# A decoder layer in three-product fp32: one set of PSUM pools to the end, output tiles paired q with 4 + q, second norm two products later, operands ahead of weight parts, three parts ahead

## The chip, the cores and the metric

The kernel runs on one core of a Trainium2 chip. The metric is the device time of one launch in microseconds (us), the median over several runs. Engines are called as the profile calls them: PE is TensorE (matmuls), PEld its weight loads, DVE is VectorE, ACT is ScalarE, POOL is GpSimd, SP the engine that issues the DMAs. SBUF is the on-chip memory; PSUM holds eight banks of 128 x 512 fp32 into which PE writes its sums.

## The reference

One hybrid decoder layer on x of 1024 positions by 1024 channels, everything in fp32:

```python
def layer(x, ...):
    h = x + hybrid_mixer(rms_norm(x, norm1_g), w_in, conv_w, conv_norm_g, ret_norm_g, w_out)
    h = h + sq_relu_mlp(rms_norm(h, norm2_g), w_up, w_down)
    return rms_norm(h, final_norm_g)

def hybrid_mixer(u, w_in, conv_w, conv_norm_g, ret_norm_g, w_out):
    z = u @ w_in                                  # 1024 x 3584
    # 512 columns: short causal convolution, gated, group norm
    # 4 heads of 128: rotary, chunkwise retention, norm, swish gate
    return concat([y_conv, y_ret], -1) @ w_out    # 1024 x 1024

def sq_relu_mlp(u, w_up, w_down):                 # 1024 -> 4096 -> 1024
    hdn = relu(u @ w_up)
    return (hdn * hdn) @ w_down
```

## The kernel before

**Precision.** Every large matmul runs on operands that are split in two: hi is the value rounded to the matmul's fp32r type, lo is the rest. A product is hi x hi + hi x lo + lo x hi, so three matmuls (128 x 128 times 128 x 512) where one would do. On top of that the large products are done by Strassen's scheme in Winograd's form: seven products of half the size in place of eight, at the price of additions before (on operands) and after (on results).

**Weights.** A weight piece `r` (128 x 4 x 128) comes by DMA from SP's queue. `split_piece` (line 168) makes two tiles of it: `wh`, a cast on ACT, and `wl`, the difference `r - wh`, on DVE (on POOL in part of the first stage). Both come from a pool `wp` of four buffers each. `prepare()` (line 180) takes the next entry of a list and appends the finished piece to `parts`; each product pops one. How many pieces are split ahead of the product that uses them is set by the early calls `prepare(2)` (lines 297 and 381): four ahead, which is as many as there are buffers. One product of 12 matmuls uses one piece.

**Order.** Each engine executes its own list in the order in which the program emits it; the order is written out by hand through a planner that estimates each engine's clock (`Engine`, `slot`, `tick`), and after a product's matmuls the program emits what the other engines do with it.

**Output projection (`group(j)`, line 1060).** Four groups j, each with output tiles j and 4 + j, eight steps. A step has 12 matmuls into one bank from `pm` or `pr`, four banks each. `out_evac` adds the finished bank into `x2[i]` (DVE, `x <- x,b`), squares it into the sums of the second norm, and begins the normalised operand `un[i]`. `group_todo` lists what else is emitted: the operands `U` of the up-projection and Strassen's sums on them. `prepare` stands at steps 4 to 7, ahead of `out_evac`.

**Change of pools.** After the fourth group the pools `pm` and `pr` are closed and three others take the eight banks: `pu` (two, up products), `pd` (four, down products), `pn` (two: the rows `r_half` of the second norm, kept through the MLP).

**MLP.** 64 up-projection row tiles are made in pairs of products. 14 early products (line 1251, `at` = 0 to 13) come first, two pairs interleaved; beside them the list `rest` emits what is left of the operands. `token_roots`, `rnorms` and `spread` turn the sums of squares into `r_half`; until then finished results wait. Then come the cycles of `jobs` (line 1301): up products (line 403, `b <- U,wh`) alternate with down products (line 1277, `b <- V,wh`), 12 matmuls each. An up result goes through relu, square and the norm factor (tiles `t`, on DVE, ACT and POOL) and becomes the operand `V` of a down product. `down_take` adds a finished down bank into quarters of `x2`.

**Pairs of output tiles.** Strassen's scheme for the down-projection is kept in a basis in which two output tiles form a 2 x 2 block: `x2[2q]` and `x2[2q+1]`. `new_basis(i)` (line 1004) changes the residual into that basis with two subtractions on POOL. Since SBUF is full, finished tiles are written out to DRAM (`put_aside`) and read again (`fetch_back`). `new_basis(1)` runs among the output groups, `new_basis(7)`, `(5)` and `(3)` at early products 7, 8 and 9, on tiles read back.

**End.** After the last cycle the basis is changed back and the last piece of the down-projection is done without Strassen (`last_mm`, line 1382), into four banks `zs` from `pn`, `pr` and `pm`; then the final norm.

Of the kernel before, what the change touches and what calls it, by code (L numbers as in the profile page):

```python
# [40 lines left out]
IN_END = [22, 23]  # L41
# [38 lines left out]
def hybrid_layer(  # L80
# [29 lines left out]
    banks_ = ctx.enter_context(ExitStack())  # L110
    pm = banks_.enter_context(tc.tile_pool(name="pm", bufs=4, space=PSUM))
    pr = banks_.enter_context(tc.tile_pool(name="pr", bufs=4, space=PSUM))
# [268 lines left out]
    prepare(2)  # L381
# [529 lines left out]
    for half in range(2):  # L911
        for f, (z, banks, pieces) in ends.items():
            for c in range(2):
# [8 lines left out]
                if half:  # L922
                    prepare()
# [80 lines left out]
    def new_basis(i):  # L1004


        for f, part in ((i - 1, hs[1]), (i, hs[0])):
            pool.tensor_sub(x2[f][:, part], x2[f][:, part], x2[i][:, hs[1]])
# [29 lines left out]
    def group_todo(j):  # L1038
# [12 lines left out]
        if j < 3:  # L1051
# [5 lines left out]
            todo[15] = [lambda: put_aside(4 + j)]  # L1057
        return todo

    def group(j):  # L1060
# [3 lines left out]
        for s, (i, c, half) in enumerate(steps):  # L1064
# [13 lines left out]
            if half:  # L1078
                prepare()
            if c:  # L1080
                out_evac(i, half, banks[i, half])
            for t in todo.get(8 * j + s, []):
                t()
            if s == 2 and j in (1, 2):
                down.fetch(4)
# [6 lines left out]
    todo[16] += [lambda: new_basis(1)]  # L1092
    todo[17] += [lambda: put_aside(0), lambda: put_aside(1)]
    todo[24] += [lambda: put_aside(2)]
    for j in range(4):
        group(j)
    banks_.close()
    pm = ctx.enter_context(tc.tile_pool(name="pu", bufs=2, space=PSUM))
    pr = ctx.enter_context(tc.tile_pool(name="pd", bufs=4, space=PSUM))
    pn = ctx.enter_context(tc.tile_pool(name="pn", bufs=2, space=PSUM))  # L1100
# [131 lines left out]
    def lo22(j):  # L1232
# [3 lines left out]
        todo[32] + call(hi22, 3),  # L1236
        todo[33] + todo[34] + hi("t2", 3),
        lo("t2", dve, 3) + hi("t3", 3) + call(lo22, 3),
# [4 lines left out]
        call(new_basis, 7),  # L1243
        call(new_basis, 5),
        call(new_basis, 3),
        [lambda: v_split(early, 1, 0)],
        [lambda: v_split(early, 1, 1)],
        [],
        [],
    ]  # L1250
    for at, (n, p) in enumerate((n, p) for n in MLP_ORDER for p in range(EARLY)):
# [3 lines left out]
        prepare()  # L1255
        for f in rest[at]:
            f()
        put_now()
        early[p].take(n, b)
        if at == 3:  # L1260
            roots = [token_roots([sums_[h]], rtok[:, 4 * h : 4 * h + 4]) for h in range(2)]
        if at == 5:
            wides = [rnorms(r) for r in roots]
        if at == 8:
            r_half[:] = [spread(w, pn) for w in wides]
# [14 lines left out]
    def down_take(n, h, bs):  # L1280
        for i, b in enumerate(bs):
            q = 2 * h + i
            quads = [x2[2 * q + f][:, sl] for f in range(2) for sl in hs]
# [17 lines left out]
    def jobs(b, old, new):  # L1301

        todo = []
        for k, n in enumerate(DOWN_ORDER):
# [8 lines left out]
            if b == NBLK - 2:  # L1313
# [3 lines left out]
                if k == 6:  # L1317
                    for q in range(4):
                        x = x2[2 * q + 1]
# [28 lines left out]
    for q in range(4):  # L1348
        pool.tensor_add(x2[2 * q][:, hs[1]], x2[2 * q][:, hs[1]], x2[2 * q + 1][:, hs[1]])
# [3 lines left out]
    TE = T - P  # L1353
# [210 lines left out]
```

## Time and profile before

| | |
|---|---|
| median of 3 runs | 1070.92 us (1070.82 to 1071.99) |
| profiled execution | 1070.03 us |
| its span | 1068.1 us |
| PE busy | 1054.8 us, 99% of the span, 4860 matmuls |
| DVE busy | 870.8 us, 82% |
| POOL busy | 561.6 us, 53% |
| ACT busy | 463.6 us, 43% |
| granted clock of PE | 9 tenths or more in each of 40 slices |

The span is one profiled execution from its first to its last instruction; the two microseconds beside it are in no row. PE is busy in 99% of the span, and its matmuls are pipelined: one starts about 0.23 us after the one ahead of it, although each lasts 0.39 us. So a delay is read from the distance of starts: two successive rows of one matmul each that start more than 0.23 us apart have a gap between them. A row with x2 or x3 merges successive matmuls.

The stages on the time axis: input projection, convolution and retention up to about 330 us, output projection 330 to 432, early MLP products 432 to 470, cycles of up and down products 470 to 1011, last down piece and final norm to 1068.

### The profile page before, as it was taken

Reading aid. Unit: us, or ns where it says so; the run is one execution under the profiler, and the core shown is the slowest. Engines: PE = TensorE matmul, PEld = TensorE weight load, DVE = VectorE, ACT = ScalarE, POOL = GpSimd, SP = SyncE. Lnnn points to the kernel's source line nnn. Section 1 sums busy time; section 2 is a strip of 40 time slices with the busy share of each in tenths; the row PEclk is TensorE's granted clock in tenths of the full one; section 3 lists DMA queues with packets and bytes.
Section 4 is the critical chain, followed back from the end, with each engine's and each line's share of the span. In section 5 each row is a group of like instructions: output and inputs, shape, how many; then the busy total and the mean of one; then the engine's idle time right before and its main releaser. Section 6 shows DMA issues by size and latency. Waiting matters only on the chain.

```text
span 1068.1 us, 13853 instructions
## 1 busy us (share of the span) xinstructions
PE 1054.8 (99%) x4860; PEld 879.2 (82%) x4860; DVE 870.8 (82%) x1231; ACT 463.6 (43%) x906; POOL 561.6 (53%) x381
## 2 busy tenths in 40 slices
PE   9999999999999999999999999999999999999997
PEld 8888888788888888788788888888888888888886
DVE  7446546799998665799999989999899899899955
ACT  8211445673437444443343433343443434334453
POOL 6334324367854233559458267277186295384552
PEclk9999999999999999999999999999999999999999
DMA  7121122122223733051221211211301201200204
GB/s 276 65 58 42 38 80 70 63 95 80 69 69 129 256 115 123 11 187 39 61 59 49 79 31 50 90 30 50 99 21 50 89 21 49 90 21 19 69 30 158
DMA packets 39685, 82.25 MB, mean 77 GB/s; under 512 B 4544, under 2 KB 5696, under 8 KB 39616
## 3 DMA queue, kind: packets, MB, share of 16 engines
q1 hardware_dynamic: 39328, 80.85, 23.5%
q8 instruction: 38, 0.62, 0.2%
q10 hardware_dynamic: 288, 0.52, 0.1%
q14 instruction: 31, 0.25, 0.1%
HBM read 71.92 MB, written 9.44 MB: 76 GB/s over the span
## 4 chain that ended last, share of the span: by engine, by line
PE 90%; DVE 6%; ACT 2%; issue 1%; POOL 1%; DVEq 0%; ACTq 0%; POOLq 0%
PE b L403 55%; PE b L1277 23%; PE b L357 4%; PE b L1386 4%; DVE t L74 1%; DVE wl L74 1%; DVE x L74 1%; DVE m L74 1%; ACT h L74 1%; DVE q L74 1%; DVE V L74 1%; PE b L339 0%; PE b L595 0%; PE b L1436 0%; PE b L246 0%
## 5 line engine op out<-in xcount | busy, mean ns | idle before, releaser
L74 ACT CAST wh<-r 128x512 fp32r<-128x512 f32 x286 | 176.6, 620 | 326.4 <-PE b L403 134.4
L403 PE MATMUL b<-U,wh 128*128 128x512 f32 x1024 | 315.8, 390 | 2.0 <-DVE x L74 1.2
L74 DVE TENSOR_TENSOR wl<-r,wh 128x512 fp32r<-128x512 f32 x250 | 232.8, 933 | 89.0 <-ACT wh L74 87.8
L74 POOL TENSOR_TENSOR r<-r,r 128x512 f32<-128x512 f32 x136 | 210.2, 1548 | 114.1 <-DVE wl L74 66.1
L1277 PE MATMUL b<-V,wh 128*128 128x512 f32 x784 | 242.0, 389 | 0.7 <-POOL V L74 0.4
L403 PEld LDWEIGHTS b<-U,wh 128*128 128x128 f32 x1024 | 191.7, 188 | 43.2 <-issue 2.4
L74 DVE TENSOR_TENSOR x<-x,b 128x512 f32<-128x512 f32 (+1 forms) x312 | 195.5, 673 | 28.8 <-PE b L1386 14.3
L403 PE MATMUL b<-U,wl 128*128 128x512 f32 x512 | 199.2, 389 | 0.0
L1277 PEld LDWEIGHTS b<-V,wh 128*128 128x128 f32 x784 | 147.1, 188 | 32.4 <-POOL V L74 0.9
L74 POOL TENSOR_TENSOR t<-t,t 128x512 f32<-128x512 f32 x70 | 106.3, 1523 | 96.4 <-ACT t L74 50.4
L1277 PE MATMUL b<-V,wl 128*128 128x512 f32 x392 | 152.5, 389 | 0.0
L74 POOL TENSOR_TENSOR wl<-r,wh 128x512 fp32r<-128x512 f32 x36 | 51.4, 1432 | 119.3 <-ACT wh L74 116.5
L403 PEld LDWEIGHTS b<-U,wl 128*128 128x128 f32 x512 | 96.1, 188 | 19.9
L403 PE MATMUL b<-uh,wh 128*128 128x512 f32 x304 | 102.3, 396 | 0.0
L403 PE MATMUL b<-ul,wh 128*128 128x512 f32 x304 | 100.5, 390 | 0.0
L403 PE MATMUL b<-uh,wl 128*128 128x512 f32 x304 | 100.2, 389 | 0.0
L1277 PEld LDWEIGHTS b<-V,wl 128*128 128x128 f32 x392 | 73.6, 188 | 15.2
L74 POOL TENSOR_TENSOR V<-t,V 128x512 fp32r<-128x512 f32 x35 | 49.6, 1418 | 67.0 <-ACT V L74 67.0
L74 DVE TENSOR_TENSOR t<-t,b 128x512 f32<-128x512 f32 x112 | 75.8, 677 | 1.7 <-POOL t L74 1.2
L74 ACT ACTIVATE t<-t 128x512 f32<-128x512 f32 x64 | 40.2, 631 | 81.2 <-DVE t L74 80.5
L74 DVE TENSOR_TENSOR V<-t,V 128x512 fp32r<-128x512 f32 x63 | 70.3, 1116 | 0.0
L403 PEld LDWEIGHTS b<-uh,wl 128*128 128x128 f32 x304 | 57.0, 188 | 12.3
(177 smaller groups left out, 1431.3 us busy)
## 6 DMA issues: line engine op xcount, KB each, us to landing
r<-w_up_t SPq DMA_DIRECT2D x64, 256.0 KB, 2.6
r<-w_down_t SPq DMA_DIRECT2D x56, 256.0 KB, 2.7
r<-w_in_t SPq DMA_DIRECT2D x48, 256.0 KB, 2.7
xt<-xT SPq DMA_DIRECT2D x16, 256.0 KB, 5.4
xs<-xT SPq DMA_DIRECT2D x8, 512.0 KB, 5.0
r<-w_out_t SPq DMA_DIRECT2D x16, 256.0 KB, 2.7
x<-xT SPq DMA_DIRECT2D x8, 512.0 KB, 7.9
k<-x SPq DMA_DIRECT2D x6, 512.0 KB, 3.0
```

Source lines behind the costliest of these rows:

```text
L74: return f(out, *args, **kw)
L357: nc.tensor.matmul(vb[i], a[k][:, i * P : (i + 1) * P], b[k // 2][:, vs], start=(k == 0 and a is uh and b is vh), stop=(k == KT - 1 and a ...
L403: nc.tensor.matmul(b, a[:, k, :], rhs(n, k)[r], start=(start and i == 0), stop=(stop and i == len(ops) - 1),)
L1277: nc.tensor.matmul(b, a, r, start=(i == 0), stop=(i == len(ops) - 1))
L1386: nc.tensor.matmul(z, a, b, start=(k == 0 and t == 0), stop=(k == 3 and t == 2))
```

## The change

Five things, in one diff.

1. `pm` and `pr` stay open to the end. The rows `r_half` take two of `pm`'s four banks from early product 9 until `r_half.clear()` behind the last cycle; the up products use the other two, the down products `pr`. The last piece's `zs` and the end's sums take banks of `pm`.
2. Output tiles q and 4 + q are paired, not 2q and 2q + 1. Tiles j and 4 + j come out of the same group, so `new_basis(j)` for j < 3 is emitted at the end of the stage of group j + 1, and both tiles are put aside after it. Only `new_basis(3)` is left to the early products. The host's layout of `w_down` and `down_take` follow.
3. The second norm's `token_roots`, `rnorms` and `spread` come two, two and one early products later.
4. In the output groups and the early products the operands (`out_evac`, `todo`, `rest`) are emitted ahead of `prepare`, and `prepare` comes in the groups at steps 0, 4, 5 and 6. The list `rest` is dealt out anew over the first three early products.
5. `prepare(2)` on line 381 becomes `prepare()`: three weight parts are split ahead, with four buffers as before. At the end of the input projection one call is moved to the first product and the last one goes.

```diff
@@ -107,9 +107,8 @@
     mixer = ctx.enter_context(ExitStack())
-    banks_ = ctx.enter_context(ExitStack())
-    pm = banks_.enter_context(tc.tile_pool(name="pm", bufs=4, space=PSUM))
-    pr = banks_.enter_context(tc.tile_pool(name="pr", bufs=4, space=PSUM))
+    pm = ctx.enter_context(tc.tile_pool(name="pm", bufs=4, space=PSUM))
+    pr = ctx.enter_context(tc.tile_pool(name="pr", bufs=4, space=PSUM))
     tp = mixer.enter_context(tc.tile_pool(name="tp", bufs=6))
@@ -378,7 +377,7 @@
     once = [token_norms]
-    prepare(2)
+    prepare()
@@ -919,7 +918,8 @@
                 slot()
-                if half:
+
+                if (f, c) == (IN_END[0], 0) if half == 0 else (f, c) != (IN_END[-1], 1):
                     prepare()
@@ -1001,11 +1001,11 @@
-    def new_basis(i):
-
-
-        for f, part in ((i - 1, hs[1]), (i, hs[0])):
-            pool.tensor_sub(x2[f][:, part], x2[f][:, part], x2[i][:, hs[1]])
+    def new_basis(j):
+
+
+        for f, part in ((j, hs[1]), (4 + j, hs[0])):
+            pool.tensor_sub(x2[f][:, part], x2[f][:, part], x2[4 + j][:, hs[1]])
@@ -1054,7 +1054,8 @@
             todo[14] = lo_of("t4")
-            todo[15] = [lambda: put_aside(4 + j)]
+            todo[14] += [lambda: new_basis(j)]
+            todo[15] = [lambda: put_aside(j), lambda: put_aside(4 + j)]
         return todo
@@ -1075,12 +1076,12 @@
             slot()
-            if half:
-                prepare()
             if c:
...
                 t()
+            if s == 0 or half and s < 7:
+                prepare()
             if s == 2 and j in (1, 2):
@@ -1089,15 +1090,8 @@
             todo.setdefault(8 * j + at, []).extend(fs)
-    todo[16] += [lambda: new_basis(1)]
-    todo[17] += [lambda: put_aside(0), lambda: put_aside(1)]
-    todo[24] += [lambda: put_aside(2)]
     for j in range(4):
         group(j)
-    banks_.close()
-    pm = ctx.enter_context(tc.tile_pool(name="pu", bufs=2, space=PSUM))
-    pr = ctx.enter_context(tc.tile_pool(name="pd", bufs=4, space=PSUM))
-    pn = ctx.enter_context(tc.tile_pool(name="pn", bufs=2, space=PSUM))
@@ -1233,36 +1227,36 @@
     rest = [
-        todo[32] + call(hi22, 3),
-        todo[33] + todo[34] + hi("t2", 3),
-        lo("t2", dve, 3) + hi("t3", 3) + call(lo22, 3),
+        todo[32] + todo[33][:1] + todo[34] + hi("t2", 3),
+        lo("t2", dve, 3) + call(hi22, 3),
+        todo[33][1:] + call(lo22, 3) + hi("t3", 3),
         call(sum4, 3) + lo("t3", dve, 3) + hi("t4", 3) + call(fetch_back, 0, 1),
...
         [],
-        call(new_basis, 7),
-        call(new_basis, 5),
         call(new_basis, 3),
+        [],
+        [],
+        [],
         [lambda: v_split(early, 1, 0)],
         [lambda: v_split(early, 1, 1)],
-        [],
         [],
...
             up.fetch(4)
-        prepare()
         for f in rest[at]:
             f()
+        prepare()
         put_now()
         early[p].take(n, b)
-        if at == 3:
+        if at == 5:
             roots = [token_roots([sums_[h]], rtok[:, 4 * h : 4 * h + 4]) for h in range(2)]
-        if at == 5:
+        if at == 7:
             wides = [rnorms(r) for r in roots]
-        if at == 8:
-            r_half[:] = [spread(w, pn) for w in wides]
+        if at == 9:
+            r_half[:] = [spread(w, pm) for w in wides]
         while r_half[0] is not None and waiting:
@@ -1280,7 +1274,7 @@
             q = 2 * h + i
-            quads = [x2[2 * q + f][:, sl] for f in range(2) for sl in hs]
+            quads = [x2[4 * f + q][:, sl] for f in range(2) for sl in hs]
             for to, op in {
@@ -1316,7 +1310,7 @@
                     for q in range(4):
-                        x = x2[2 * q + 1]
+                        x = x2[4 + q]
                         four[q].append(
@@ -1346,11 +1340,12 @@
     for q in range(4):
-        pool.tensor_add(x2[2 * q][:, hs[1]], x2[2 * q][:, hs[1]], x2[2 * q + 1][:, hs[1]])
+        pool.tensor_add(x2[q][:, hs[1]], x2[q][:, hs[1]], x2[4 + q][:, hs[1]])
...
     TE = T - P
+    r_half.clear()
     ssq3, R3 = unit(s="ssq"), unit(s="R3")[:, :H]
@@ -1402,7 +1397,7 @@
         if n == H:
-            zs[:4] = [bank(p_) for p_ in (pn, pn, pr, pm)]
+            zs[:4] = [bank(p_) for p_ in (pm, pm, pr, pm)]
             for k in range(4):
@@ -1425,7 +1420,7 @@
-    ends = [bank(pn) for _ in range(2)]
+    ends = [bank(pm) for _ in range(2)]
     sums = cp.tile([P, 3], F32, name="sums")
@@ -1537,7 +1532,7 @@
         .reshape(NBLK - 1, 2, 2, P, 2, 2, 2, P)
-        .transpose(0, 6, 2, 4, 3, 5, 1, 7)
+        .transpose(0, 4, 2, 5, 3, 6, 1, 7)
         .reshape(NBLK - 1, 4, 2, P, 4, P),
```

What this does to the order on three engines is shown in three places.

DVE at the end of the output projection, before. The rows are the evacuations of the last two banks of the output groups (`x <- x,b`; `b_3804` is the very last), the operands `U` and `un` of the up-projection, and weight parts `wl`:

```order
L74 TENSOR_TENSOR wl_3839<-r_3408,wh_3838 128x512
L74 TENSOR_TENSOR x_3165<-x_3165,b_3782 128x512
L74 TENSOR_TENSOR U_3823<-un_3583,U_3823 128x512
L74 TENSOR_TENSOR wl_3864<-r_3592,wh_3863 128x512
L74 TENSOR_TENSOR x_3169<-x_3169,b_3804 128x512
L74 TENSOR_TENSOR wl_3909<-r_3406,wh_3908 128x512
L74 TENSOR_TENSOR un_3755<-un_3755 128x512
L74 TENSOR_TENSOR wl_3935<-r_3590,wh_3934 128x512
L74 TENSOR_TENSOR U_3915<-un_3755,U_3915 128x512
L74 SCALAR_TENSOR_TENSOR un_3755<-x_3169,sm,un_3755 128x512 x2
```

and after:

```order
L74 TENSOR_TENSOR x_3159<-x_3159,b_3782 128x512
L74 TENSOR_TENSOR U_3819<-un_3581,U_3819 128x512
L74 TENSOR_TENSOR wl_3847<-r_3408,wh_3846 128x512
L74 TENSOR_TENSOR x_3163<-x_3163,b_3804 128x512
L74 TENSOR_TENSOR un_3755<-un_3755 128x512
L74 TENSOR_TENSOR U_3895<-un_3755,U_3895 128x512
L74 SCALAR_TENSOR_TENSOR un_3755<-x_3163,sm,un_3755 128x512
L74 TENSOR_TENSOR wl_3902<-r_3590,wh_3901 128x512
L74 TENSOR_TENSOR U_3899<-un_3755,U_3899 128x512
L74 TENSOR_TENSOR wl_3927<-r_3406,wh_3926 128x512
```

In both lists one weight part stands ahead of the last evacuation. Behind it stood a weight part, `un`, another weight part and then the operand `U`; now `un` and `U` come first, and the weight parts behind them.

POOL in the early MLP, before. `r` are Strassen's sums on weights, `x <- x,x` and `x <- x` the two subtractions of a `new_basis`, `V` the first operand of a down product:

```order
L74 TENSOR_TENSOR r_3410<-r_3412,r_3406 128x512
L74 TENSOR_TENSOR r_3594<-r_3596,r_3590 128x512
L74 TENSOR_TENSOR x_4037<-x_4037,x_3169 128x512
L74 TENSOR_TENSOR x_3169<-x_3169 128x512
L74 TENSOR_TENSOR x_4033<-x_4033,x_4035 128x512
L74 TENSOR_TENSOR x_4035<-x_4035 128x512
L74 TENSOR_TENSOR x_4031<-x_4031,x_3165 128x512
L74 TENSOR_TENSOR x_3165<-x_3165 128x512
L74 TENSOR_TENSOR V_4214<-t_3997,V_4214 128x512
```

and after:

```order
L74 TENSOR_TENSOR r_3410<-r_3412,r_3406 128x512
L74 TENSOR_TENSOR r_3592<-r_3594,r_3588 128x512
L74 TENSOR_TENSOR x_3159<-x_3159,x_3163 128x512
L74 TENSOR_TENSOR x_3163<-x_3163 128x512
L74 TENSOR_TENSOR V_4216<-t_3985,V_4216 128x512
L74 TENSOR_TENSOR r_3890<-r_3890,r_3892 128x512
```

Six subtractions, of which some need tiles read back (`x_4031` to `x_4037` are such), have become two on tiles that were never put aside; the others stand among the output groups.

POOL in the last cycle, before, where `V` are operands of the last down products and `r` sums on the last weights:

```order
L74 TENSOR_TENSOR V_8512<-t_8014,V_8512 128x512
L74 TENSOR_TENSOR t_7969<-t_7969,t_8014 128x512
L74 TENSOR_TENSOR r_8463<-r_8463,r_8509 128x512
L74 TENSOR_TENSOR r_8320<-r_8463,r_8320 128x512
L74 TENSOR_TENSOR r_8417<-r_8417,r_8320 128x512
L74 TENSOR_TENSOR V_8606<-t_8157,V_8606 128x512
```

and after:

```order
L74 TENSOR_TENSOR V_8495<-t_7998,V_8495 128x512
L74 TENSOR_TENSOR t_7952<-t_7952,t_7998 128x512
L74 TENSOR_TENSOR V_8588<-t_8140,V_8588 128x512
L74 TENSOR_TENSOR r_8468<-r_8468,r_8519 128x512
L74 TENSOR_TENSOR r_8329<-r_8468,r_8329 128x512
L74 TENSOR_TENSOR r_8425<-r_8425,r_8329 128x512
```

The operand `V` that stood behind three sums on weights stands ahead of them.

## Rows read from the trace of the kernel before

**Rows 1.** The page's busy times: us, share of the span, instructions

```profile
PE 1054.8 (99%) x4860; PEld 879.2 (82%) x4860; DVE 870.8 (82%) x1231; ACT 463.6 (43%) x906; POOL 561.6 (53%) x381
```

**Rows 2.** Timeline of PE, 431-437: start, us, engine, line, operation [idle before <-releaser]

```profile
431.79 0.39 PE L403 MATMUL b<-yh,wl 128*128 128x512 f32 x1
432.64 0.70 PE L403 MATMUL b<-U,wh 128*128 128x512 f32 x2 [0.47 <-DVE x L74]
...
435.23 0.39 PE L403 MATMUL b<-U,wl 128*128 128x512 f32 x1
436.31 0.70 PE L403 MATMUL b<-U,wh 128*128 128x512 f32 x2 [0.70 <-DVE x L74]
```

**Rows 3.** Timeline of DVE, 431 to 436

```profile
431.21 0.69 DVE L74 TENSOR_TENSOR wl<-r,wh 128x512 fp32r<-128x512 f32 x1 [0.55 <-ACT wh L74]
...
434.32 1.24 DVE L74 TENSOR_TENSOR wl<-r,wh 128x512 fp32r<-128x512 f32 x1 [0.46 <-ACT wh L74]
435.49 0.67 DVE L74 TENSOR_TENSOR x<-x,b 128x512 f32<-128x512 f32 x1
```

**Rows 4.** Timeline of PE, 496 to 516

```profile
496.94 0.39 PE L1277 MATMUL b<-V,wl 128*128 128x512 f32 x1
497.37 0.70 PE L403 MATMUL b<-U,wh 128*128 128x512 f32 x2
...
510.87 0.39 PE L403 MATMUL b<-U,wl 128*128 128x512 f32 x1
511.47 0.70 PE L1277 MATMUL b<-V,wh 128*128 128x512 f32 x2 [0.22 <-DVE x L74]
...
514.05 0.39 PE L1277 MATMUL b<-V,wl 128*128 128x512 f32 x1
515.18 0.71 PE L403 MATMUL b<-U,wh 128*128 128x512 f32 x2 [0.74 <-ACT t L74]
```

**Rows 5.** POOL's groups, 430-520: busy us, mean ns of one | idle before <-releaser

```profile
L74 POOL TENSOR_TENSOR x<-x 128x512 f32<-128x512 f32 x3 | 4.8, 1586 | 0.0
L74 POOL TENSOR_TENSOR x<-x,x 128x512 f32<-128x512 f32 x3 | 4.3, 1445 | 11.7 <-DMA x<-k 11.7
```

**Rows 6.** Timeline of all engines, 473 to 478

```profile
473.49 1.73 POOL L74 TENSOR_TENSOR V<-t,V 128x512 fp32r<-128x512 f32 x1
...
478.12 0.39 PE L1277 MATMUL b<-V,wh 128*128 128x512 f32 x1
```

**Rows 7.** Windows: us, busy of PE, PEld, DVE, ACT, POOL; PEclk, DMA share, GB/s

```profile
320.00:430.00 110.00, 110.00 (x487) 91.06 (x487) 73.21 (x96) 58.49 (x96) 39.78 (x28) 1.00 0.45 151
...
478.00:516.00 38.00, 36.99 (x162) 29.74 (x161) 36.68 (x47) 14.70 (x26) 32.90 (x22) 1.00 0.11 35
554.00:592.00 38.00, 38.00 (x169) 31.45 (x169) 37.46 (x49) 15.05 (x28) 30.43 (x20) 1.00 0.13 37
```

**Rows 8.** Timeline of PE near the end of the MLP, 978 to 980

```profile
978.67 0.39 PE L1277 MATMUL b<-V,wh 128*128 128x512 f32 x1
979.50 0.50 PE L1277 MATMUL b<-V,wh 128*128 128x512 f32 x1 [0.44 <-POOL V L74]
```

**Rows 9.** Timeline of all engines at the start of the last piece, 1011 to 1013

```profile
1011.38 0.84 PE L1386 MATMUL b<-hid,wd 128*128 128x512 f32 x3
1011.83 0.69 DVE L74 SCALAR_TENSOR_TENSOR t<-t,b 128x512 f32<-128x512 f32 x1
...
1012.57 1.67 PE L1386 MATMUL b<-hid,wd 128*128 128x512 f32 x6 [0.35 <-DVE t L74]
```

**Rows 10.** Waits of all engines: us in total, times, longest

```profile
ACT wh L74 <- PE b L403: 134.4, 72, 4.8
```

**Rows 11.** Timeline: a weight part and its first matmul, 520 to 524, 595 to 600

```profile
520.47 1.71 DVE L74 TENSOR_TENSOR wl<-r,wh 128x512 fp32r<-128x512 f32 x1
...
523.90 0.39 PE L1277 MATMUL b<-V,wl 128*128 128x512 f32 x1
...
595.19 1.73 DVE L74 TENSOR_TENSOR wl<-r,wh 128x512 fp32r<-128x512 f32 x1
...
600.06 0.39 PE L1277 MATMUL b<-V,wl 128*128 128x512 f32 x1
```

## The prediction

> **What bounds the kernel now.** I read the busy times first: PE is busy 1054.8 us of a span of 1068.1 [rows 1]. What a change of order can win are the gaps in PE's own list, and there are not many. So the second view is PE's timeline, in which I looked for matmuls that start later than they should. How far apart they should start is read from a row of three that runs without a stop: it lasts 0.84, one matmul lasts 0.39, so each starts 0.225 behind the one ahead [rows 9, 2]. A row of two should then last 0.615; behind a stop it lasts 0.70, so the restart itself costs another 0.085 [rows 2]. A product of 12 matmuls is 12 x 0.225 = 2.7 us; that is the unit in which everything is moved here.
>
> The gaps that lie where the change edits are three groups.
>
> A, the change of pools. 431.79 to 432.64 is 0.85; less 0.225, plus the restart, 0.71. 435.23 to 436.31 is 1.08, so 0.94 in the same way [rows 2]. Together 1.65. Both waits are put down to DVE's `x`, the evacuation of a bank of the output projection: the first products of the MLP write into banks of new pools, which are free only when the old pools' last banks have been read. The very last evacuation starts at 435.49, behind a weight part of 1.24 from 434.32 [rows 3], and ends at 436.16; PE starts again at 436.31.
>
> B, the first cycle. 496.94 to 497.37: 0.29; 510.87 to 511.47: 0.46; 514.05 to 515.18: 1.00, all worked out as above [rows 4]. Together 1.75. The releasers are DVE's `x`, that is a bank that was not yet evacuated, and ACT's `t`, an activation that follows DVE. From 478 to 516 DVE is busy 36.68 of 38.00 and PE loses 1.01; from 554 to 592 DVE is busy even 37.46 of 38.00 and PE loses nothing [rows 7]. So a full DVE alone does not stop PE. What stops it is that DVE comes into the first cycle with a backlog and cannot work it off.
>
> C, the end. 978.67 to 979.50 is 0.83, the next interval begins with a matmul of 0.50 in place of 0.39: 0.83 - 0.225 + 0.11 = 0.72, and the releaser is POOL's `V` [rows 8]. The first row of the last piece starts at 1011.38 with three matmuls, so the fourth was due at 1012.06; it starts at 1012.57 and its row of six lasts 1.67 in place of 0.39 + 5 x 0.225 = 1.52: 0.51 + 0.15 = 0.66, released by DVE's `t` of 1011.83 [rows 9].
>
> A + B + C = 1.65 + 1.75 + 1.38 = 4.78 us. That is the most that this change can win; the rest of the gaps lie in stages that it does not touch.
>
> **The change part by part.** *Pools kept open.* The first MLP products then take the banks of `pm` and `pr` in their turn, and those which the first two products get were emptied a group earlier than the last evacuation. A goes entirely: -1.65. Bounds 0 (some other bank or operand is as late) and -1.65. What could be late next is the operand `U` of the second product; in the list of DVE it now stands second behind the last evacuation, not fourth, because the two weight parts of 0.69 to 1.24 us between them have gone behind it [rows 3]. I take -1.65. In the cycles the two banks of `r_half` come out of `pm`, two are left to the up products and four to the down products, just as before, so PE's 38.00 of 38.00 there stays as it is [rows 7].
>
> *New pairs.* Before, POOL does six subtractions of `new_basis` in the early MLP: 4.8 + 4.3 = 9.1 us, behind 11.7 us of waiting for the tiles that are read back [rows 5]. Two of them stay there (3.0 us, by the mean of both kinds), and without the wait, since tiles 3 and 7 are not put aside. Four go to the output projection, 6.1 us. There POOL is busy 39.78 of 110 and DVE 73.21 of 110, and PE is full [rows 7]: the 6.1 us hide in 70 of POOL's idle time; if that cover were gone the whole 6.1 would be the price. Their two put-aside DMAs per group stand in SP's queue behind the subtractions; raw pieces are ordered several products ahead, so I cost that at nothing, with a bound of +1.0 for one late piece.
>
> What the early stage wins is less POOL work beside DVE. A weight part on DVE lasts 0.69 by itself and up to 1.71 or 1.73 in the cycles [rows 3, 11], where POOL is busy 30.43 of 38.00 [rows 7]: about 1.0 more where the two meet. Four subtractions less, each able to lengthen one DVE instruction by 1.0, is at most 4 us of DVE's backlog; about half of DVE's instructions read PSUM and hardly suffer, so 2 us. The gaps of B sum to 1.75 and come out of one backlog, so 2 us might close all. But the second part of the list `rest` and the norm are also rearranged, and DVE stays at 97% there [rows 7]. I take -1.2 of -1.75, bounds 0 and -1.75.
>
> The Trainium skill speaks of just this meeting ("SBUF — State Buffer", section "SBUF: two separate sides"): VectorE with two SBUF inputs and GpSimd reading SBUF share a pair of ports as an exclusive lock, and the one that comes second is blocked until the first is done. By the trace a DVE instruction of 0.69 becomes 1.71, which is 1.02 more, less than the whole 1.45 to 1.59 of a POOL subtraction [rows 3, 5, 11]. By the rule, each subtraction taken away gives DVE its full length, 6.1 us, and B would go wholly: 0.55 less than my sum. By the same rule the four in the output projection block DVE for up to 6.1 us, out of 36.8 that it is idle there.
>
> *Second norm two products later.* The first operand `V` of the down products is made one product later. Before, POOL starts it at 473.49 right behind the subtractions and is done at 475.22; PE wants it at 478.12, 2.9 later [rows 6]. Moved by 2.7 with nothing ahead of it on POOL, it keeps most of this. Cost 0, bounds 0 and +2.7 (a whole product late, if POOL is as late as before).
>
> *Operands ahead of weight parts; three ahead.* A weight part is needed one product, 2.7 us, sooner after it is emitted. The smallest slack in a quiet cycle: the part from 595.19 ends at 596.92, PE uses it at 600.06, 3.14 later; 2.7 less leaves 0.44. In the first cycle the part from 520.47 ends at 522.18 and is used at 523.90: 1.72, so 1.0 too late if DVE is not earlier [rows 11]. Against it, ACT's casts now wait for a buffer 134.4 us in 72 waits, 1.9 on average, until a product is done with it [rows 10]; with three ahead one buffer is free when the cast is emitted, that wait goes, and DVE's difference behind it is never held. Nothing is to be won by that in itself, since PE is full in the cycles. Bounds 0 and +6 (1.0 in each of six later cycles); I take +0.4, near the row that leaves 0.44, for one late part of 1.0 in the first cycle that comes four times in ten.
>
> *End.* In the list of POOL the `V` that is late in [rows 8] stands ahead of three sums on weights: -0.72. The last piece's second bank was one from which DVE still reads at 1011.83 [rows 9]; it now comes out of `pm`, where results were taken earlier: -0.66. Bounds 0 and -1.38; I take all.
>
> Sum: -1.65 - 1.2 - 1.38 + 0.4 = -3.83. Against the profiled execution's 1070.03 (span 1068.1, the rest beside it) that is 1066.2. The median of the runs is 1070.92, 0.89 above the profiled one, so the same kernel in the median comes to **1067.1**.
>
> **The rivals.** What a measurement of this kernel can tell from no change is 0.2%, 2.14 us: faster is below 1068.78, slower above 1073.06.
>
> *The same: the backlog stays.* For it: DVE is at 97 to 99% through the cycles, and the 9.1 us of POOL are little in the 32.90 of 38.00 that it is busy up to 516 [rows 7]. Against it: B has gaps that no later cycle has. Then A goes, of C the half, B stays and a late part of 1.0 is added: -1.65 - 0.69 + 1.0 = -1.3, or **1069.6**.
>
> *Slower: weight parts too late.* The mechanism is DVE's `wl` behind longer POOL work, emitted one product nearer to its use. It decides from the point where DVE's `wl` ends less than 2.7 us ahead of its matmul by the old count. The row of 1.72 is below this, that of 3.14 just above [rows 11]; 0.44 of slip is enough. If in each of the first cycle and five more one part is 1.0 late, PE loses 6; A and half of C still go: +6 - 1.65 - 0.69 = +3.7, **1074.6**. Against it: the operands now ahead of the part make DVE's order earlier for those, and the part later, by some 0.7 for each of them; the freed buffer takes away ACT's wait.
>
> *The banks bring nothing.* With `r_half` in `pm`, or because the operand `U` is as late as the bank was, A stays in other places: B and C alone give -1.2 - 1.38 + 0.4 = -2.2, **1068.7**, just faster. The blocking rule named above is no case of its own: its time, 1066.5, lies in the forecast's range.
>
> **How the numbers follow.** The forecast, with its own range 1065.9 to 1068.7: 0.54. Banks bring nothing: 0.10, half of it on either side of the bound. The backlog stays: 0.20, within the bound. Weight parts too late: 0.13. The V operand late by 2.7 with the rest as forecast, 1069.8: 0.03. Faster is 0.54 + 0.05 = 0.59, same 0.20 + 0.05 + 0.03 = 0.28, slower 0.13. The range reaches down to all gaps closed, 1070.92 - 4.78 = 1066.1, less 0.5 for gaps elsewhere that shift: 1065.6. Up it goes to 1071.2, the backlog's 1069.6 with a second and a third of C's and B's terms not coming true (1.6 more). Outside are the slower case and little else.
>
> **What would show it.** Right: PE's starts at the first two up products follow each other at 0.225 (A); POOL has two subtractions in the early MLP and no wait for a read-back, and the gaps near 497, 511 and 515 shrink to under 0.6 together (B); `V` near 978 ahead of the sums, and no gap behind the third matmul of the last piece (C); ACT's wait for PE's products falls from 134.4 to a small part. Wrong: waits of PE for DVE's `wl`, above all in the quiet cycles, or a PE that is no longer 38.00 of 38.00 there.

## The result, and the profile after

The changed kernel takes 1074.98 us (median of 9 runs, 1072.51 to 1076.79), the kernel before 1071.02 (9 runs). The ratio is 1.0035, with an interval from 1.0027 to 1.0044: slower by 0.35%, where 1067.1 was forecast. The time is near that of the rival "weight parts too late" (1074.6), but the places are others than that rival named.

The profiled execution is the slowest of the nine. Its span is 1073.88, 5.74 more than before. The page's busy times, answering to [rows 1]:

```profile
PE 1057.5 (98%) x4860; PEld 881.5 (82%) x4860; DVE 870.5 (81%) x1233; ACT 461.9 (43%) x906; POOL 557.4 (52%) x379
```

No engine has more to do; the 2.7 that PE has more, and the 2.3 of PEld, go with the clock (below). So the time is in waits and in what the clock makes of the matmuls behind them. PE's waits in the changed kernel (line waited, releaser: us in total, times, longest; line 402 is line 403 of before, 1271 is 1277):

```profile
PE b L402 <- DVE wl L74: 3.2, 3, 2.0
PE b L662 <- ACT h L74: 2.2, 5, 0.7
PE b L402 <- ACT wh L74: 2.1, 2, 1.2
```

Before, PE never waited for a weight part. Now it waits for `wl` and `wh`; the only other new wait, 0.5 for `vh`, lies in the first 6 us, and the waits for banks are gone. Since both kernels issue 4860 matmuls, the time between two numbers in PE's own list can be compared stage by stage. I take it from the starts in the traces, from the profiled executions:

| from matmul to matmul | before | after | difference |
|---|---|---|---|
| first to 25th (from the span's start) | 6.48 | 6.92 | +0.44 |
| 25th to 1,201st | 233.32 | 233.15 | -0.17 |
| 1,201st to 1,401st, end of the input projection | 45.33 | 49.41 | +4.08 |
| 1,401st to 2,041st | 145.07 | 145.07 | 0 |
| 2,041st to 2,301st, last output product and early MLP | 56.99 | 61.71 | +4.72 |
| 2,301st to 4,301st, cycles | 455.13 | 453.33 | -1.80 |
| 4,301st to 4,860th, end | 118.56 | 116.84 | -1.72 |

The sum is +5.55; 0.19 are behind the last matmul. The +4.72 contain what A won, 1.65, so the early MLP lost 6.4.

**What was won.** PE's timeline at the change from output projection to MLP, and at the first row of the last piece:

```profile
436.13 0.39 PE L402 MATMUL b<-yh,wl 128*128 128x512 f32 x1
436.36 0.62 PE L402 MATMUL b<-U,wh 128*128 128x512 f32 x2
...
1017.59 1.75 PE L1381 MATMUL b<-hid,wd 128*128 128x512 f32 x7
```

436.13 to 436.36 is 0.23 where [rows 2] have 0.85, and the seven matmuls of the last piece run through (0.39 + 6 x 0.225 = 1.74) where [rows 9] stop after three. The cycles have no gap either; windows of the changed kernel, answering to [rows 7]:

```profile
554.00:592.00 38.00, 38.00 (x169) 31.45 (x169) 34.11 (x44) 14.22 (x25) 31.39 (x21) 1.00 0.08 22
478.00:516.00 38.00, 38.00 (x170) 31.45 (x169) 35.19 (x45) 15.51 (x27) 33.43 (x22) 1.00 0.07 22
```

PE is busy 38.00 of 38.00 in both. A, B and C are closed.

**What was lost, first place: 261 us, in the input projection.** PE's timeline there:

```profile
261.10 0.62 PE L402 MATMUL b<-U,wh 128*128 128x512 f32 x2
263.73 0.55 PE L402 MATMUL b<-U,wl 128*128 128x512 f32 x1 [2.02 <-DVE wl L74]
264.08 1.05 PE L402 MATMUL b<-U,wh 128*128 128x512 f32 x2
```

A `wl` is 2.02 late. What stood ahead of it, from the timeline of the other engines:

```profile
251.55 1.74 POOL L74 TENSOR_TENSOR a<-a,z 128x512 f32<-128x512 f32 x1
...
253.36 1.62 POOL L74 TENSOR_TENSOR a<-a,ssq 128x512 f32<-128x512 f32 x1
...
254.94 6.52 POOL L74 TENSOR_TENSOR r<-r,r 128x512 f32<-128x512 f32 x4
...
261.49 0.62 ACT L74 CAST wh<-r 128x512 fp32r<-128x512 f32 x1 [1.08 <-POOL r L74]
261.93 3.42 DVE L74 TENSOR_TENSOR wl<-r,wh 128x512 fp32r<-128x512 f32 x2
```

The cast waits for POOL's `r`, Strassen's sums on weights, and DVE's difference waits for the cast. Before, the same four sums ran here on POOL:

```profile
250.51 6.40 POOL L74 TENSOR_TENSOR r<-r,r 128x512 f32<-128x512 f32 x4
```

They start 4.43 later now, 4.2 of it beside the 0.27 by which the kernel is later at its 1,201st matmul. A part that is emitted one product later takes its sums on weights with it, and the planner gave POOL two additions `a` ahead of them: 251.55 to 254.94, or 3.39 of the 4.43. Before, DVE did two such at 250.03 and 251.13. A chain of four sums and two splits behind each other has no slack left.

**Second place: 428 to 457 us, the early MLP.** Timeline of all engines:

```profile
428.85 0.73 ACT L74 ACTIVATE U<-x,sm 128x512 fp32r<-128x512 f32 x1 [3.41 <-PE b L402]
...
437.70 1.30 POOL L74 TENSOR_TENSOR t<-t,t 128x512 f32<-128x512 f32 x1 [6.17 <-ACT t L74]
...
438.96 1.75 POOL L74 TENSOR_TENSOR x<-x,x 128x512 f32<-128x512 f32 x1
...
440.66 1.75 POOL L74 TENSOR_TENSOR x<-x 128x512 f32<-128x512 f32 x1
...
442.37 5.33 POOL L74 TENSOR_TENSOR r<-r,r 128x512 f32<-128x512 f32 x3
...
444.69 0.62 ACT L74 CAST U<-un 128x512 fp32r<-128x512 f32 x1 [2.78 <-DVE un L74]
445.22 0.61 ACT L74 CAST wh<-r 128x512 fp32r<-128x512 f32 x1
...
445.88 0.73 PE L402 MATMUL b<-U,wh 128*128 128x512 f32 x2 [1.20 <-ACT wh L74]
```

Three things are to be seen. The subtractions of `new_basis(2)` do not lie among the output groups: POOL comes to them at 438.96, when the MLP has begun, and the sums `r` stand behind them. In POOL's list they stand behind a sum of squares `t`, ahead of which POOL is idle for 6.17: the idle time was there, but the pair stands behind it. (A kernel with the pair ahead of this `t` was not tried.) ACT waits 3.41 for PE before it can write an operand `U`. And the weight's cast at 445.22 stands behind an operand's cast that waits 2.78 for DVE. Which of these makes PE wait is not to be read from the trace; the experiments tell.

**The clock.** Behind both places the granted clock falls, windows of the changed kernel:

```profile
264.00:267.30 3.30, 3.30 (x9) 2.57 (x9) 3.27 (x4) 1.77 (x3) 3.09 (x3) 0.51 0.40 150
455.00:458.30 3.30, 3.21 (x8) 2.54 (x9) 2.69 (x6) 1.98 (x4) 0.03 (x1) 0.53 0.02 5
```

At 0.51 to 0.53, which is the level of 1.2 GHz, matmuls start 0.427 apart, not 0.225. There are 8 such in the first place and 7 in the second, so 1.6 of the 4.08 and 1.4 of the 6.4 are the clock. The nine runs differ by how much of this they had: the run with a mean clock of 0.999 took 1072.51, the three with 0.995 took 1075.65 to 1076.79.

### The profile page after: what moved, and what is told of

It reads as the page before. It is cut to its first block, busy times and chain, and to the rows that moved or that the text cites. A ratio compares the mean times of both kernels' runs of the same rounds, so it can differ in the third digit from the quotient of the medians.

```text
span 1073.9 us, 13771 instructions
## 1 busy us (share of the span) xinstructions
PE 1057.5 (98%) x4860; PEld 881.5 (82%) x4860; DVE 870.5 (81%) x1233; ACT 461.9 (43%) x906; POOL 557.4 (52%) x379
## 4 chain that ended last, share of the span: by engine, by line
PE 88%; DVE 4%; ACT 3%; POOL 2%; issue 2%; DMA 0%; SPq 0%; DVEq 0%; POOLq 0%; ACTq 0%
PE b L402 53%; PE b L1271 25%; PE b L356 4%; PE b L1381 4%; ACT h L74 1%; DVE m L74 1%; POOL r L74 1%; DVE q L74 1%; PE b L338 0%; POOL a L74 0%; DVE h L74 0%; PE b L1431 0%; DMA wv<-w_v 0%; POOL x L74 0%; DVE out L74 0%
## 5 line engine op out<-in xcount | busy, mean ns | idle before, releaser
L74 POOL TENSOR_TENSOR r<-r,r 128x512 f32<-128x512 f32 x136 | 206.9, 1525 | 130.4 <-DVE wl L74 74.3
L74 DVE TENSOR_TENSOR wl<-r,wh 128x512 fp32r<-128x512 f32 x247 | 221.9, 901 | 44.3 <-ACT wh L74 44.0
L74 POOL TENSOR_TENSOR wl<-r,wh 128x512 fp32r<-128x512 f32 x39 | 55.9, 1435 | 122.6 <-ACT wh L74 104.0
L74 DVE TENSOR_TENSOR V<-t,V 128x512 fp32r<-128x512 f32 x63 | 73.5, 1167 | 0.0
```

The costliest lines, as they stand in the source:

```text
L74: return f(out, *args, **kw)
```

## The experiments

All ratios are against the kernel before, run on the same chip (1070.86 to 1071.73 in its medians). "Early" is the stage from matmul 2,041 to 2,301 in the profiled execution: 56.99 before, 61.71 after. Where a part of it ran at half clock, the text says how much that made, at 0.2 for each matmul; where it says nothing, none did.

**Four weight parts ahead.** The changed kernel, with

```diff
-    prepare()
+    prepare(2)
...
-                if (f, c) == (IN_END[0], 0) if half == 0 else (f, c) != (IN_END[-1], 1):
+                if half:
                     prepare()
...
-            if s == 0 or half and s < 7:
+            if half:
                 prepare()
```

> The changed kernel with four weight parts ahead again (and with it the calls of prepare at the end of the input projection and at steps 4 to 7 of a group, still behind the operands). Everything else as changed. Theory DEPTH (three ahead is the cause of both new stalls, near 261 and 444 to 457): both go, nothing is at half clock behind them, the time is 1071.0 less the 5.0 of the gaps that the change closes, 1066.0. Rival ORDER (in the early MLP the weight parts come late because they are queued behind the operands, whatever their number): the stall near 261 goes (3.7 us), the one at 444 to 457 stays (6.2 us): 1071.3. Rival POOL (the sums on weights come late behind a basis subtraction): as ORDER.

1071.17, ratio 1.0003 (0.9994 to 1.0011). The input projection is back at 45.33. The early stage keeps 59.25, with these waits of PE:

```profile
PE b L402 <- ACT wh L74: 1.4, 1, 1.4
PE b L402 <- DVE wl L74: 1.4, 2, 1.0
```

So depth explains the first place, and of the second only 2.46, 1.4 of which are the clock. DEPTH, which had both go, failed; ORDER and POOL, which gave the same time, are not told apart here.

**Three ahead, in the kernel before.** The reverse of that diff.

> The kernel before with three weight parts ahead and the places of prepare that go with it, nothing else of the change. DEPTH: a stall of about 2 us near 261 with a stretch of half clock behind it (3.7 in all) and one in the early MLP of 4 to 6: 1071.0 + 8 to 10 = 1079 to 1081, less nothing. ORDER or POOL: only the one near 261: 1074.7.

1073.33, ratio 1.0024 (1.0010 to 1.0038). The gap near 261 appears (2.15), with no loss in the early stage (56.04, even 0.95 less than before). A wait that neither theory named stands in the first cycle, at 512.66, where the prediction's rival had put one of 1.0:

```profile
PE b L403 <- DVE wl L74: 3.5, 2, 2.0
```

Of its two, one is the 2.0 at 261 and the other the 1.5 there. The cycles take 458.01, 2.88 more than before, 1.6 of it at half clock. And with nothing else changed the end takes 116.82, as in the changed kernel: three ahead by itself gives all of C.

**Weight parts ahead of the operands in the early MLP, three ahead.**

```diff
+        prepare()
         for f in rest[at]:
             f()
-        prepare()
         put_now()
```

> The changed kernel with prepare ahead of the operands again in the 14 early products of the MLP, three ahead as changed. ORDER: the stall at 444 to 457 goes, that near 261 stays: 1075.0 - 6.2 = 1068.8. DEPTH: it stays for the most part, above 1073. POOL: it stays as it is, 1075.

1072.88, ratio 1.0016 (1.0007 to 1.0025). The early stage is 59.00, as with four ahead; of the 2.71 less, 1.4 are the clock. ORDER by itself, which had the whole stall go, has failed too.

**The pools alone, on the kernel before.**

```diff
-    pm = banks_.enter_context(tc.tile_pool(name="pm", bufs=4, space=PSUM))
+    pm = ctx.enter_context(tc.tile_pool(name="pm", bufs=4, space=PSUM))
...
-    banks_.close()
-    pm = ctx.enter_context(tc.tile_pool(name="pu", bufs=2, space=PSUM))
...
-            r_half[:] = [spread(w, pn) for w in wides]
+            r_half[:] = [spread(w, pm) for w in wides]
...
```

> The kernel before with the two PSUM pools kept to the end, nothing else of the change. By the prediction's steps: the gaps at 432 and 436 (1.65) and the one at the start of the last piece (0.66) go, the rest stays: 1071.0 - 2.3 = 1068.7. Rival (the banks bring nothing, another wait takes their place): 1071.0.

1070.51, ratio 0.9995 (0.9985 to 1.0004), not to be told from before. A is gone, but PE, 1.65 earlier, comes to an operand that is not ready:

```profile
447.22 0.40 PE L402 MATMUL b<-U,wh 128*128 128x512 f32 x1
448.76 0.51 PE L402 MATMUL b<-U,wh 128*128 128x512 f32 x1 [1.14 <-DVE U L74]
```

That gives 1.3 back, and 1.0 more at 497. The 0.6 of the last piece stay won (end 117.95).

**Four ahead, and weight parts first.** Both edits above on the changed kernel.

> The changed kernel with four weight parts ahead and, in the 14 early products, prepare ahead of the operands again. With four ahead alone, or prepare first alone, the part for early product m is emitted at the same place among the operands (behind those of product m - 4); with both it is emitted one product earlier, as in the kernel before. PLACE (what counts is that place in the lists of ACT and DVE): the stall of 3.3 us that four ahead alone left at 443 to 450 goes, 1071.2 - 3.3 = 1067.9. POOL (the two basis subtractions in front of the sums on weights are the cause): it stays, 1071.2.

1074.26, ratio 1.0027 (1.0016 to 1.0037): the opposite of PLACE, and above POOL's 1071.2 too. The waits for weight parts are gone, and PE waits for operands instead:

```profile
PE b L402 <- ACT U L74: 3.3, 1, 3.3
...
PE b L402 <- DVE U L74: 1.8, 1, 1.8
```

The early stage takes 63.20, the worst of all, 2.0 of it by half clock. As far as these runs tell, weight parts and operands are two users of ACT and DVE that are late together, and the order chooses only which of them stops PE.

**The third basis change later, four ahead.**

```diff
-            todo[14] += [lambda: new_basis(j)]
+            if j < 2:
+                todo[14] += [lambda: new_basis(j)]
...
         call(new_basis, 3),
-        [],
+        call(new_basis, 2),
```

> The changed kernel with four weight parts ahead and new_basis(2) moved from the last output group to early product 8, on tiles read back. POOL: with its two subtractions (3.0 us) out of the way the sums on weights come 3 us earlier and DVE's operands no longer lie beside them; the stall at 443 to 450 shrinks from 3.3 to under 1, 1068.5. PLACE: it keeps at least 2.5 of its 3.3, 1071.

1067.40, ratio 0.9966 (0.9953 to 0.9979). Early 56.30, cycles 453.56. Moving one pair of subtractions, 3.0 us on POOL, was worth 3.8 between the medians. The largest gap that is left in the early stage is 0.57. ACT's operand `U` (the one that waited at 428.85) in this kernel:

```profile
420.79 0.72 ACT L74 ACTIVATE U<-x,sm 128x512 fp32r<-128x512 f32 x1
```

and with four ahead but `new_basis(2)` in its place:

```profile
425.15 0.73 ACT L74 ACTIVATE U<-x,sm 128x512 fp32r<-128x512 f32 x1 [3.41 <-PE b L402]
```

The lists of ACT and DVE are the same in both up to this instruction. What differs for this instruction is the buffer that the operand was given, by the program's addresses. In the first the operand lies where output tile 2 lay, which is put aside at once; in the second, tile 2 must wait for its basis change, and the operand lies where an operand `y` lay, from which PE still reads.

**Pairs alone, on the kernel before.** The second of the five changes only.

> The kernel before with tiles q and 4 + q paired (subtractions among the output groups, host layout, put-asides), nothing else of the change. By the prediction's step B: of the gaps at 497, 511 and 515 (1.75) 1.2 go, 1069.8. Rival (the two subtractions that fall on the start of the early MLP make weight parts or operands late there): a new gap of 1 to 3 at 440 to 455, 1071 to 1073.

1073.49, ratio 1.0019 (1.0010 to 1.0028). The cycles take 453.33, exactly as in the changed kernel. This does not yet show that B's gain comes from the pairs, since here too PE stands in front of the cycles, where DVE can catch up: the early stage takes 61.11:

```profile
PE b L403 <- DVE x L74: 3.6, 2, 2.9
```

With pools that change, DVE's lateness is paid at the banks (a gap of 3.10 at 432.59, before the place that the rival named).

**Pools and pairs, on the kernel before.**

> The kernel before with both the pools kept and tiles q and 4 + q paired; four ahead, weight parts ahead of operands, order of the operands and the norm as before. If the gains add (pools alone was 0.7 under before, with a new wait of 1.3 for the operand U at 447 and one of 1.2 at 497): the gap at 497 and those at 511 and 515 go, the one at 447 stays, 1071.0 - 1.65 - 0.66 - 1.75 + 1.3 = 1068.2. If the subtractions do harm at the start of the MLP: 1070 or more.

1072.62, ratio 1.0013 (1.0004 to 1.0022). The gains do not add: early 61.22, 1.6 of it by half clock, now with a wait of 3.0 for POOL's sum of squares `t`, at the norm's matmuls:

```profile
PE b L312 <- POOL t L74: 3.0, 1, 3.0
```

**The third basis change later, three ahead.** The changed kernel with only that edit.

> The changed kernel (three ahead) with new_basis(2) moved to early product 8, nothing else. The same move with four ahead gave 1067.4. If three ahead costs only the stall near 261 (2.1 of waiting and up to 1.6 of half clock): 1069.5 to 1071.1, and nothing over 0.7 at 440 to 457. Rival (three ahead also makes weight parts late in the early MLP, whatever POOL does): a stall of 2 to 3 there as well, 1073 to 1074.

1072.75, ratio 1.0005 (0.9995 to 1.0014), between the two theories. Input projection 49.47 with the clock low again, early 57.71: three ahead costs 1.4 there even with POOL free.

**POOL's time without the buffer.** Four ahead, `new_basis(2)` later, and in its old place

```diff
+            else:
+                todo[14] += [lambda: pool.tensor_sub(sums_[0], sums_[0], sums_[1])]
+                todo[14] += [lambda: pool.tensor_add(sums_[0], sums_[0], sums_[1])]
```

> The changed kernel with four ahead and new_basis(2) at early product 8, and in its old place in the last output group two POOL instructions of the same size that change nothing (a sum of squares less and plus another one). Moving new_basis(2) did two things: it took 3.0 us from POOL ahead of the sums on weights, and it let tile 2 be put aside early, so that the operand U for x2[3] gets tile 2's buffer and not that of an operand y which PE still reads (ACT waited 3.4 us for PE there). POOL TIME: the stall at 443 to 450 comes back, 1067.4 + 3.5 = 1070.9. BUFFER: ACT's wait for PE stays away and the stall too, 1067.4 to 1068.

1069.72, ratio 0.9984 (0.9975 to 0.9993), between both theories. Early 58.24: of the 2.95 between 56.30 and 59.25, POOL's time makes 1.94, and the rest, 1.01, is put down to the buffer. Here the operand has tile 2's buffer again, and ACT does not wait for PE there. A cast of `U` that ACT makes just before PE's 2,041st matmul comes 1.19 ahead of that matmul (at 429.78), as it does without the two instructions (428.81); with the buffer of `y` it comes only 0.05 ahead (430.79). The medians, each against before on its chip (0.9966, 0.9984, 1.0003), divide the loss about equally, 1.9 for POOL's time and 2.0 for the buffer. So both causes are shown, and their shares only roughly. PE's timeline shows which gap is whose:

```profile
443.43 0.39 PE L402 MATMUL b<-U,wl 128*128 128x512 f32 x1
444.23 0.73 PE L402 MATMUL b<-U,wh 128*128 128x512 f32 x2 [0.41 <-ACT wh L74]
445.99 0.50 PE L402 MATMUL b<-U,wl 128*128 128x512 f32 x1 [1.02 <-DVE wl L74]
```

The wait for `wh` is 0.41, as without the two instructions (1.42 with the buffer); the wait of 1.02 for `wl` is back.

**Pools and pairs, third basis change later.** The edit of two experiments back, on pools and pairs.

> The kernel before with the two pools kept, tiles q and 4 + q paired and new_basis(2) at early product 8; four ahead, weight parts ahead of the operands, operands and norm in the places of before. If the order of operands and weight parts is worth nothing: as the changed kernel with four ahead and this move, 1067.4. If it is worth what pools alone lost to the late operand U at 447 and at 497 (1.3 and 1.0): 1069.7.

1068.34, ratio 0.9968 (0.9956 to 0.9981). Early 56.79, cycles 453.66, where the pools alone had 456.20: with no stall in front of them the cycles win 2.5 by the pairs. A wait of 1.14 for `U` near 447 is there, that near 497 is not; against 1067.40 (0.9966) this is no difference. Operands ahead of weight parts, the later norm and the new `rest` take that wait away and are worth no more than the measurement can tell.

**Four ahead, three from the cycles on.** With `new_basis(2)` later, and

```diff
-        prepare()
+        if at < 13:
+            prepare()
```

> The changed kernel with four ahead up to the early products, three from the first cycle of up and down products on (one prepare less at the last early product), and new_basis(2) at early product 8. With four all the way it gave 1067.4 and had one gap left of 0.6 near 978, where V stood behind sums on weights. Three ahead puts V in front of these and had, in the changed kernel, no wait of PE between 458 and 1011. QUIET CYCLES HOLD: 1067.4 - 0.6 = 1066.8, no new gap. RIVAL (the slowdown that was feared in the prediction, weight parts 1.0 late in the first cycle and after): 1068.4 or more, with waits of PE for wl after 480.

1067.88, ratio 0.9971 (0.9958 to 0.9983). The end takes 116.84, 1.05 less than with four; the cycles take 1.24 more:

```profile
507.55 0.61 PE L402 MATMUL b<-U,wh 128*128 128x512 f32 x2
509.00 0.50 PE L402 MATMUL b<-U,wl 128*128 128x512 f32 x1 [0.84 <-DVE wl L74]
```

The rival held in the first cycle, and nowhere after it. The best version is the one with four ahead and the third basis change later, 0.34% faster than before (0.9966, 0.9953 to 0.9979), with two others that cannot be told from it.

## Why the prediction was wrong, step by step

**A, -1.65: right in the changed kernel, not by the pools alone.** The gaps are closed, and no bank is waited for. But pools alone were worth nothing that could be measured: the operand `U`, which the prediction named as "what could be late next" and priced at nothing, takes 1.3 of it. The changed order of operands, with the later norm and the new `rest`, is what keeps it away: the wait stands in pools and pairs with the third basis change later, and not in the changed kernel with four ahead and the same move.

**B, -1.2 of 1.75: right, and more.** The cycles won 1.80. That the pairs do it is shown where no stall stands in front of the cycles: 453.56 and 453.66 with the third basis change later and four ahead, against 455.13 before. Yet with three ahead, and again no long stall, 1.0 comes back in the first cycle (the last experiment). In the changed kernel DVE had 6 us of lost time of PE to catch up in; its clean first cycle was, as far as this tells, partly paid for by the stall before.

**C, -1.38: right, 1.72.** That is above the step's bound: a gap of 0.29 at 957, which the prediction had not listed, went as well. The reasons were mixed up, though: three ahead gives both parts by itself (116.82), and the 0.6 of the last piece come with the pools alone too (117.95).

**Second norm two products later, 0: right.** In the changed kernel PE does not wait for `V`.

**New pairs, cost at nothing: this step failed.** The prediction said that four subtractions "go to the output projection", where "the 6.1 us hide in 70 of POOL's idle time". Two do. The pair of `new_basis(2)` is emitted in the last group, and POOL reaches it at 438.96, in the early MLP, in front of the sums on weights on which the next casts wait. An average over 110 us says nothing on the last 10 of them, where POOL's idle time stands ahead of the pair and not behind it. And the step counted only POOL's time; that both tiles must be kept until their basis changes, so that an operand gets a buffer which PE still reads, was not counted at all. Measured, with four ahead: 2.95 in the profiled stage, 1.94 for POOL's time and 1.01 for the buffer; 3.8 between the medians, about half for each.

**Three ahead, +0.4: this step failed.** It was priced from the "smallest slack in a quiet cycle" and the first cycle. The quiet cycles were right: PE is busy in all of 38.00 there. The input projection, where four sums on weights stand ahead of two splits, was not looked at; it cost 4.08, or 2.30 where the clock stayed. In the early MLP three ahead cost 1.4 with POOL free, and 2.46 (61.71 - 59.25, of which 1.4 are the clock) with POOL late. A part that is emitted one product later was taken to be 2.7 later at its use and no more, whereas its sums `r`, and what the planner puts ahead of them, move too.

Also wrong: ACT's wait for PE's products at line 403 did not fall "to a small part" of 134.4. In the kernel before, the wait at the down products, and both in the changed kernel:

```profile
ACT wh L74 <- PE b L1277: 121.3, 74, 2.4
...
ACT wh L74 <- PE b L402: 133.4, 74, 4.8
ACT wh L74 <- PE b L1271: 51.3, 47, 2.4
```

What fell, by 70.0, is the wait at the down products.

**The sum.** Won: 1.65 + 1.80 + 1.72 = 5.17, against 4.23 forecast. Lost: 4.08 + 6.37 = 10.45, against 0.4; 3.0 of it are the clock, which the prediction did not count. What was won is above the 4.78 that it called the most. The rest, 0.27 by its stages and 0.19 at the tail, is the scatter of the start and the end (to the 25th matmul the profiled executions take from 6.29 to 7.56). **The rival "slower" had the mechanism (a `wl` or `wh` that is late) and by chance its size, but not the place:** "the first cycle and five more" lost nothing in the changed kernel.

What stays open is why the planner lets POOL do the two additions `a` ahead of the sums near 251; a kernel with three ahead and these on DVE was not tried.

## What to carry to other kernels

When fewer parts are prepared ahead, look for the price where the chain that makes a part is longest, not where the machine is fullest: the quiet cycles, to which the prediction left 0.44 of slack, lost nothing, while the stage with four sums ahead of the casts lost 4. Work that is moved "into" a stage must be placed on the time axis of the engine that does it, with what stands behind it in that engine's list, and what its tiles keep occupied is part of its price. And when a gap is closed, look for the next operand: pools alone closed 1.65 and lost 1.3 at the next operand and 1.0 more in the cycles.

## What the runs showed of the hardware

**The clock does not answer to the same wait in the same way.** A gap of 2.0 us near 261 is followed by a granted clock of 0.51 in the changed kernel, and by 1.00 in the kernel before with three ahead:

```profile
261.00:263.50 2.50, 0.54 (x2) 0.48 (x3) 2.50 (x3) 0.34 (x1) 2.42 (x2) 1.00 0.00 0
263.50:267.00 3.50, 3.50 (x17) 2.87 (x16) 3.46 (x4) 1.77 (x3) 3.29 (x3) 1.00 0.59 154
```

The stage takes 49.41 in the one and 47.63 in the other, so the same gap costs 2.3 or 4.1. Pairs alone has a longer gap, 3.10 at 432.59, and full clock behind it. The longest distance of two starts in the kernel before is 1.13 [rows 4], and its mean clock is 0.998 or 0.999 in every run beside the experiments; that of the changed kernel goes from 0.995 to 0.999.

**DVE and POOL: whoever starts first is not slowed.** With the two idle instructions, POOL's `r` starts at 444.11 and takes 1.28; DVE's `wl` starts 0.10 behind it and takes 1.72:

```profile
444.11 1.28 POOL L74 TENSOR_TENSOR r<-r,r 128x512 f32<-128x512 f32 x1
444.21 1.72 DVE L74 TENSOR_TENSOR wl<-r,wh 128x512 fp32r<-128x512 f32 x1 [1.21 <-ACT wh L74]
```

Without them the same `wl` starts first and takes 0.69, and POOL's `r`, 0.02 behind it, takes 1.82:

```profile
443.24 0.69 DVE L74 TENSOR_TENSOR wl<-r,wh 128x512 fp32r<-128x512 f32 x1 [1.21 <-ACT wh L74]
443.26 1.82 POOL L74 TENSOR_TENSOR r<-r,r 128x512 f32<-128x512 f32 x1
```

This agrees with the exclusive lock of the Trainium skill ("SBUF — State Buffer", section "SBUF: two separate sides"), by which the one that starts first keeps the ports for its whole instruction. The prediction had weighed that rule for the subtractions, in the stage into which it moved them; what met the weight parts here, at the start of the MLP, are the sums `r` that stand behind the last pair.
